# Other start addresses in SBUF for the tiles of a decoder layer: three pads of new sizes

## The chip, the cores and the metric

The kernel runs on one core of a Trainium2 chip. The metric is the time of one execution on the device, in microseconds. The core has TensorE (PE in the profile; PEld is its loading of weights), VectorE (DVE), ScalarE (ACT), GpSimd (POOL) and SyncE (SP, which here only issues DMAs). They share a memory of 128 partitions, SBUF. A tile lies at the same address in every partition, and "start" below means that address in bytes, mostly modulo 512.

## The reference

One decoder layer on 1024 tokens of width 1024, all in float32:

```python
xn = rmsnorm(x, norm_mix_w)
da_q, da_k, da_v, sw_q, sw_k, sw_v, g_da, g_sw = split_cols(xn @ w_in)
y_da = diff_attention(da_q, da_k, da_v, ...)        # 4 heads, causal, ALiBi
y_sw = sliding_window_attention(sw_q, sw_k, sw_v, sinks)   # 8 heads, window 128
merged = sigmoid(g_da) * (y_da @ w_br_da) + sigmoid(g_sw) * (y_sw @ w_br_sw)
x = x + merged @ w_mix_out
x = x + conv_ffn(rmsnorm(x, norm_ffn_w), w_up, conv_w, conv_b, w_down)   # width 2816
return rmsnorm(x, norm_final_w)
```

## The kernel before

**Products.** Every large product keeps float32's accuracy with three matmuls. Weights and activations are each cut into a high part (`wh`, `xh`) and the rest (`wl`, `xl`), and `wh` x `xh`, `wh` x `xl` and `wl` x `xh` are added in PSUM (lines 150 to 152, 276 to 278, 835 to 837, 996 and 1023). A matmul streams 512 columns of the activation, the moving operand, against 128x128 weights; the weights of the next matmul are loaded while it streams. `wh` is used by two matmuls in a row and loaded for each.

**Pairs.** Two blocks of weights are often computed together by a scheme with seven products in place of eight (P1 to P7). It needs sums of weight blocks, S1 to S4, whose two parts are the tiles `sh` and `sl`, and sums of activations, T1 to T4 (`t13h`, `t42h` and so on in the projection, `T_0h` and so on later). A11, A12 and A22 are plain weight blocks, B11, B21 and B22 plain activations (`B_0h` and so on).

**Stages**, in order: the projection (`project`), attention (`attention`, with blocks of gates between its steps, `back_half`), the merge of the two branches (in `rest`, moving operands `yh`, `yl`), the mix (`mix`, operands `mh`, `ml`), the hidden stage (`hidden`, 22 pairs of blocks) and the down projection (`down`, operands `h`).

**Where tiles lie.** Pools of tiles are stacked in SBUF from two sides. The order in which the pools are opened sets the addresses. At the very bottom of each side `run` opens a pad, a pool with one tile that nothing reads or writes (lines 180 to 182; LPAD and RPAD on line 32). From the left follow constants, `rstd`, and then the pool `wp` with the weights as they are loaded (`raw`) and their two parts (`wh`, `wl`). Behind it, also from the left, come each stage's other left-hand tiles: the sums of weights of the projection, the merge's operands, the parts of the hidden stage's activations, most parts `h` of the down projection. From the right come the activations of the projection and their sums, nearly all of attention, `mh` and `ml`, and in the hidden stage and the down projection the sums of weights and some of the activations (T42 and the pool `hpb`). Nearly all of these tiles have sizes that are multiples of 512 bytes, so the tiles of one side keep one start modulo 512.

In the program built from this kernel the tiles of `wp` and the other left-hand ones start at 192 modulo 512, those from the right at 0. Slices inside a tile keep that: weights are taken in steps of 512 bytes, activations in steps of 2048.

**Order.** Each engine works through its own list. A scheduler makes the lists when the program is built, and semaphores make an engine wait for another where one needs the other's result.

Of the kernel before, what the change touches and what calls it, by code (L numbers as in the profile page):

```python
# [10 lines left out]
F32 = mybir.dt.float32  # L11
# [6 lines left out]
P = 128  # L18
# [10 lines left out]
STORE = (1,9)  # L29
DEFER = (4,8)  # L30
N1 = 6
LPAD, RPAD = 480, 480
LAM_INIT = 0.2

HALVES = ((2,), (0, 0, 0, 0, 1, 1, 0, 0), (0, 0, 0, 0, 1, 0, 0, 1), (0, 0, 0, 0, 1, 0, 1, 0), (0, 0, 0, 1, 1, 0, 1, 0), (1, 0, 0, 1, 0, 1, 1, 0), (1, 0, 1, 1, 0, 0, 1, 0), (3,))
# [7 lines left out]
class Trunk:  # L43
# [132 lines left out]
    def run(self):  # L176
        nc, tc = self.nc, self.tc
        with ExitStack() as ctx:

            for side, n in (("left", LPAD), ("right", RPAD)):  # L180
                pad = ctx.enter_context(tc.tile_pool(name=f"pad_{side}", bufs=1, side=side))
                pad.tile([P, n // 4], F32, name=f"pad_{side}_t")
            self.cp = ctx.enter_context(tc.tile_pool(name="cp", bufs=1))
            self.st = ctx.enter_context(tc.tile_pool(name="st", bufs=4))
            self.dp = ctx.enter_context(tc.tile_pool(name="dp", bufs=1, space=DRAM))
            self.ident = self.cp.tile([P, P], F32, name="ident")
            make_identity(nc, self.ident)
            self.ones = self.cp.tile([P, 1], F32, name="ones")
            nc.gpsimd.memset(self.ones, 1.0)
            self.mhalf = self.cp.tile([P, 8], F32, name="mhalf")  # L190
            nc.gpsimd.memset(self.mhalf, -0.5)
            self.vecs = self.cp.tile([P, NVEC], F32, name="vecs")

            warm = self.cp.tile([P, 1], F32, name="warm")
            nc.scalar.activation(warm, self.ones, AF.Exp)
            nc.scalar.dma_start(self.vecs, self.vecs_d)
            self.rstd = self.cp.tile([P, T], F32, name="rstd")
            self.gd = self.dp.tile([16, P, T], F32, name="gd")
            self.x2d = self.dp.tile([8, P, T], F32, name="x2d")
            self.hd = self.dp.tile([NF, P, T], F32, name="hd")  # L200
            self.yd = self.dp.tile([8, P, T], F32, name="yd")
            self.wp = ctx.enter_context(tc.tile_pool(name="wp", bufs=2))
            self.qd = self.dp.tile([18, 2, P, T], F32, name="qd")
            self.xctx = ExitStack()
            self.xp = self.xctx.enter_context(tc.tile_pool(name="xp", bufs=1, side="right", reuse_waits="tile"))
            self.plan()
            self.project()
            self.pctx = ExitStack()
            self.psS = self.pctx.enter_context(tc.tile_pool(name="psS", bufs=2, space=PSUM, reuse_waits="tile"))
            self.psG = self.pctx.enter_context(tc.tile_pool(name="psG", bufs=2, space=PSUM, reuse_waits="tile"))  # L210
            self.psT = self.pctx.enter_context(tc.tile_pool(name="psT", bufs=2, space=PSUM, reuse_waits="tile"))
            gctx = ExitStack()
            self.gpool = gctx.enter_context(tc.tile_pool(name="gp", bufs=2, reuse_waits="tile"))
            self.attention()
            self.rest(gctx)
# [995 lines left out]
```

## Time and profile before

The median of two runs is 1365.2 us (1364.79 to 1365.61). One execution was profiled; its span, from the first to the last instruction, is 1364.3 us, and no further time of that execution is given.

| stretch of the span, us | stage | PE busy, us | PE instructions | DVE busy, us | DMA share |
|---|---|---|---|---|---|
| 0 to 252 | projection | 244.85 | 1068 | 170.09 | 0.46 |
| 252 to 509 | attention | 255.10 | 1503 | 209.25 | 0.54 |
| 509 to 598 | merge | 87.81 | 382 | 44.29 | 0.44 |
| 598 to 687 | mix | 88.83 | 387 | 52.65 | 0.42 |
| 687 to 1119 | hidden | 431.30 | 1873 | 376.18 | 0.25 |
| 1119 to 1364 | down | 237.34 | 1099 | 163.39 | 0.47 |

Matmuls overlap in the pipeline and their ends are modelled, so a busy PE isn't a PE at its peak. To see how fast matmuls follow one another, look at the starts of successive ones. In the profile's rows, a line of groups has: line, engine, operation, output <- inputs (moving operand, weights), tile, form, count, then busy us and mean ns of one, then idle time before. A line of the chain has: start, duration, engine, tile, line, count.

### The profile page before, as it was taken

To read this page: it belongs to the slowest core of one execution; us is meant where nothing else is said; L and a number is where in the kernel's file an instruction comes from. 1 tells how busy PE (TensorE), PEld (TensorE's weight loads), DVE (VectorE), ACT (ScalarE), POOL (GpSimd) and SP (SyncE) were. 2 spreads that over 40 slices of the span, in tenths; PEclk is the share of its full clock that TensorE was granted. 3 is DMA by queue.
4 is the path that set the end of the run, shared out by engine and by line. 5 is a ranking of instruction groups with operands and counts; after the bars stand their busy time and mean duration, and the time that the engine had idled before them with its cause. 6 is when DMAs were issued, how large, how long until landed. Compare 5 with 4: busy or idle time off the path is not lost.

```text
span 1364.3 us, 17160 instructions
## 1 busy us (share of the span) xinstructions
PE 1345.2 (99%) x6304; PEld 1104.3 (81%) x6304; DVE 1015.9 (74%) x1454; ACT 603.9 (44%) x942; POOL 485.5 (36%) x350
## 2 busy tenths in 40 slices
PE   8999999999999999999999999999999999999997
PEld 6888888888887778878878888888888888888887
DVE  8747775388898875455689889888988888976454
ACT  8432232276667674334444333433344335332343
POOL 0336652010102135642455565556555611131011
PEclk9999999999999999999999999999999999999999
DMA  7334343966554235334522222222222238651242
GB/s 254 139 106 173 137 147 118 271 173 178 154 132 144 82 118 220 110 124 129 165 78 93 77 78 93 67 88 78 93 77 79 85 136 316 206 179 59 93 133 84
DMA packets 62469, 179.50 MB, mean 132 GB/s; under 512 B 6832, under 2 KB 15152, under 8 KB 62384
## 3 DMA queue, kind: packets, MB, share of 16 engines
q1 hardware_dynamic: 50928, 160.98, 36.5%
q10 hardware_dynamic: 11456, 17.41, 3.5%
q8 instruction: 50, 0.82, 0.2%
q14 instruction: 35, 0.29, 0.1%
HBM read 129.61 MB, written 48.76 MB: 131 GB/s over the span
## 4 chain that ended last, share of the span: by engine, by line
PE 86%; DVE 5%; POOL 3%; DMA 3%; issue 1%; ACT 1%; POOLq 0%; SPq 0%; ACTq 0%; DVEq 0%
PE t L837 14%; PE t L836 14%; PE t L835 14%; PE d L996 3%; PE y L996 3%; PE sc L568 3%; PE g L150 3%; PE g L151 3%; PE g L152 3%; DMA gr<-gd 2%; PE sc L152 2%; PE sc L150 2%; PE sc L151 2%; PE d L1023 2%; PE y L1023 2%; POOL gr L742 2%
## 5 line engine op out<-in xcount | busy, mean ns | idle before, releaser
L970 ACT ACTIVATE c<-us,vecs 128x1024 f32<-128x1024 f32 x44 | 54.7, 1246 | 162.6 <-POOL us L965 159.1
L965 POOL TENSOR_TENSOR us<-us,rstd 128x1024 f32<-128x1024 f32 x42 | 100.9, 2420 | 54.7 <-DVE wl L131 36.4
L110 ACT CAST sh<-sf 128x1024 fp32r<-128x1024 f32 x62 | 64.7, 1047 | 108.4 <-POOL sf L97 59.7
L129 ACT CAST wh<-raw 128x1024 fp32r<-128x1024 f32 (+2 forms) x60 | 60.7, 1011 | 108.6 <-PE sc L151 33.6
L131 DVE TENSOR_TENSOR wl<-raw,wh 128x1024 fp32r<-128x1024 f32 (+2 forms) x60 | 75.8, 1263 | 41.5 <-ACT wh L129 31.6
L971 DVE SCALAR_TENSOR_TENSOR c<-us,vecs,c 128x1024 f32<-128x1024 f32 x44 | 67.2, 1530 | 52.0 <-ACT c L970 52.0
L96 POOL TENSOR_TENSOR sf<-rv 128x512 f32<-128x512 f32 x30 | 43.0, 1434 | 166.6 <-DMA rv<-in_w_up 62.6
L112 DVE TENSOR_TENSOR sl<-sf,sh 128x1024 fp32r<-128x1024 f32 x62 | 90.5, 1462 | 8.6 <-ACT sh L110 8.4
L167 POOL TENSOR_TENSOR rs<-ms,mhalf 128x8 f32<-128x8 f32 (+2 forms) x9 | 14.5, 1615 | 161.2 <-DVE ms L165 150.6
L150 PE MATMUL g<-xh,wh 128*128 128x512 f32 x176 | 70.6, 401 | 0.1
L152 PE MATMUL g<-xh,wl 128*128 128x512 f32 x176 | 70.5, 401 | 0.0
L151 PE MATMUL g<-xl,wh 128*128 128x512 f32 x176 | 70.3, 399 | 0.0
L98 POOL TENSOR_TENSOR sf<-raw,rv 128x512 f32<-128x512 f32 x30 | 41.7, 1391 | 61.1 <-DVE sl L112 61.1
L572 DVE CUSTOM_DVE_ANT_0 L<-sc,bias 128x128 f32<-128x128 f32 (+7 forms) x64 | 47.7, 751 | 17.0 <-PE sc L568 13.8
L551 POOL MEMSET aT<- 128x128 f32 x32 | 6.2, 206 | 151.8 <-PE t L597 101.3
L97 POOL TENSOR_TENSOR sf<-sf,raw 128x512 f32<-128x512 f32 x31 | 58.1, 1875 | 1.7
L573 ACT ACTIVATE L<-L,sm 128x128 f32<-128x128 f32 (+7 forms) x64 | 49.6, 778 | 20.3 <-DVE sm L572 17.7
L972 DVE SCALAR_TENSOR_TENSOR c<-us,vecs,c 128x1024 f32<-128x1024 f32 x44 | 56.1, 1278 | 0.6
L725 POOL TENSOR_TENSOR gr<-gr,rstd 128x1024 f32<-128x1024 f32 x16 | 40.4, 2528 | 41.4 <-DMA gr<-gd 41.0
L112 DVE TENSOR_TENSOR wl<-raw,wh 128x1024 fp32r<-128x1024 f32 (+1 forms) x35 | 54.8, 1565 | 0.2
L150 PE MATMUL sc<-mh,wh 128*128 128x512 f32 x128 | 50.4, 394 | 0.0
L152 PE MATMUL sc<-mh,wl 128*128 128x512 f32 x128 | 50.2, 392 | 0.0
(444 smaller groups left out, 4358.8 us busy)
## 6 DMA issues: line engine op xcount, KB each, us to landing
u<-qd SPq DMA_DIRECT2D x72, 256.0 KB, 6.4
raw<-in_w_down SPq DMA_DIRECT2D x27, 512.0 KB, 3.7
raw<-in_w_in SPq DMA_DIRECT2D x25, 512.0 KB, 3.9
hr<-hd SPq DMA_DIRECT2D x50, 256.0 KB, 5.5
raw<-in_w_up SPq DMA_DIRECT2D x23, 512.0 KB, 3.5
hd<-c SPq DMA_DIRECT2D x22, 512.0 KB, 2.8
rv<-in_w_up SPq DMA_DIRECT2D x21, 512.0 KB, 3.5
gr<-gd SPq DMA_DIRECT2D x16, 512.0 KB, 3.6
```

Source lines behind the costliest of these rows:

```text
L110: nc.scalar.copy(hi, src)
L112: nc.vector.tensor_tensor(lo, src, hi.bitcast(F32), ALU.subtract)
L131: self.lo = (eng or nc.vector).tensor_tensor(wl, raw, wh.bitcast(F32), ALU.subtract)
L150: nc.tensor.matmul(ps, wh[:, kc + o, :], ah, start=first and n == 0, stop=False)
L151: nc.tensor.matmul(ps, wh[:, kc + o, :], al, start=False, stop=False)
L152: nc.tensor.matmul(ps, wl[:, kc + o, :], ah, start=False, stop=last and n == len(kcs) - 1)
L835: nc.tensor.matmul(ps, ah[:, k, :], bh, start=first and n == 0, stop=False, skip_group_check=skip)
L836: nc.tensor.matmul(ps, ah[:, k, :], bl, start=False, stop=False, skip_group_check=skip)
L837: nc.tensor.matmul(ps, al[:, k, :], bh, start=False, stop=last and n == len(ks) - 1, skip_group_check=skip)
L965: i = (nc.vector if m % NF == 0 else nc.gpsimd).tensor_tensor(us[:, 2:], us[:, 2:], self.rstd, ALU.mult)
L971: nc.vector.scalar_tensor_tensor(c, us[:, 1:T + 1], cw[1], c, ALU.mult, ALU.add)
L996: nc.tensor.matmul(ps, v[:, n, :], x, start=n == i == 0, stop=n == len(js) - 1 and i == 2)
```

## The change

Two pads get other sizes, and a third pad is opened behind `wp`, on the left. In the program built from the changed kernel the tiles of `wp` start at 0 modulo 512, the left-hand tiles of the pools behind it at 64, those from the right at 160. Constants and `rstd` move along (`rstd` from 32 to 352). The instructions of every engine, their order and what they wait for are those of the program before; the DMAs are the same too. The pads take 1184 bytes of each partition in place of 960.

```diff
-LPAD, RPAD = 480, 480
+LPAD, MPAD, RPAD = 288, 64, 832
...
             self.wp = ctx.enter_context(tc.tile_pool(name="wp", bufs=2))
+            pad = ctx.enter_context(tc.tile_pool(name="pad_middle", bufs=1))
+            pad.tile([P, MPAD // 4], F32, name="pad_middle_t")
             self.qd = self.dp.tile([18, 2, P, T], F32, name="qd")
```

## The prediction

> **What bounds the kernel now.** First the page's busy times, its slices and its chain of work.
>
> ```profile
> span 1364.3 us, 17160 instructions
> PE 1345.2 (99%) x6304; PEld 1104.3 (81%) x6304; DVE 1015.9 (74%) x1454; ACT 603.9 (44%) x942; POOL 485.5 (36%) x350
> ...
> PE   8999999999999999999999999999999999999997
> ...
> PEclk9999999999999999999999999999999999999999
> ...
> PE 86%; DVE 5%; POOL 3%; DMA 3%; issue 1%; ACT 1%; POOLq 0%; SPq 0%; ACTq 0%; DVEq 0%
> ```
>
> TensorE is busy from the first slice to the last at a granted clock of nine tenths or more, and 86% of the chain is matmuls. So the time is the number of matmuls times the distance between the starts of two of them. That distance, which I call the cadence, is what an address could change. I read it from three stretches without a wait: two from the chain in order of time (start, us, what), one from the timeline (start, us of one).
>
> ```profile
> 1263.61 5.44 PE d L996 x24
> ```
>
> ```profile
> 1121.58 2.06 PE y L1023 x9
> ```
>
> ```profile
> 956.12 0.39 PE L835 MATMUL t<-T_1h,sh 128*128 128x512 f32 x1
> ...
> 959.62 0.39 PE L835 MATMUL t<-B_2h,sh 128*128 128x512 f32 x1
> ```
>
> All three run the same instruction, 128x512 against 128x128 weights, one weight load to each matmul. The first takes 5.44/24 = 226.7 ns, the second 2.06/9 = 228.9 ns, and in the third 15 matmuls start between the two rows: 3.50/15 = 233.3 ns. What differs is where the operands lie. While a matmul streams its moving operand, the weights of the next are loaded. I call "distance" the start of those weights minus the start of the moving operand, modulo 512 bytes; slices of a weight tile are 512 bytes apart and halves of an activation 2048, so it is the same for a whole group. In the first stretch weights and moving operand both lie at 192: distance 0. In the second the weights lie at 192 and the operand at 0: +192. In the third it is the other way round: -192. The trace thus ties the cadence to the distance; it shows only these three, and the change leaves only one of them in use.
>
> The groups by line (form, count, busy, mean ns of one) show how even this is:
>
> ```profile
> L150 PE MATMUL sc<-mh,wh 128*128 128x512 f32 x128 | 50.4, 394 | 0.0
> L152 PE MATMUL sc<-mh,wl 128*128 128x512 f32 x128 | 50.2, 392 | 0.0
> L151 PE MATMUL sc<-ml,wh 128*128 128x512 f32 x128 | 49.9, 390 | 0.2
> ...
> L837 PE MATMUL t<-t13h,sl 128*128 128x512 f32 x72 | 28.4, 394 | 0.0
> L836 PE MATMUL t<-t13l,sh 128*128 128x512 f32 x72 | 28.2, 392 | 0.0
> L835 PE MATMUL t<-t13h,sh 128*128 128x512 f32 x72 | 27.9, 388 | 0.0
> ...
> L152 PE MATMUL g<-yh,wl 128*128 128x512 f32 x64 | 24.9, 389 | 0.0
> ...
> L835 PE MATMUL t<-B_0h,wh 128*128 128x512 f32 x44 | 17.4, 395 | 0.0
> ...
> L837 PE MATMUL t<-B_0h,wl 128*128 128x512 f32 x44 | 17.2, 391 | 0.0
> L836 PE MATMUL t<-B_0l,wh 128*128 128x512 f32 x44 | 17.1, 389 | 0.0
> ```
>
> A mean here is a modelled end: rows of 389 belong to stretches of 226.7, so I take some 162 off. The mix (`mh`, +192) then runs at 230 ns, the projection's sums (`t13h`, +192) at 229, the rows at distance 0 at 227 with a run-in: the first rows of a product show 395 and 391, the later ones 389, some 228 on average. Sums against left tiles (-192) run at 233.
>
> **The change part by part.** It alters three pad sizes and adds a fourth pad that no instruction touches. The lists of the two built programs have the same instructions in the same order on every engine, the same waits and the same DMAs; only start addresses differ. So nothing is removed, queued or moved past anything. In the built programs, 5240 matmuls are 512 wide. By what streams and what is loaded beside it:
>
> - wp weights beside a right-hand operand (projection, gates, mix, A22 with T4, part of the down projection): 1818, distance +192 becomes -160.
> - wp weights beside a left-hand operand (merge, P1 and P2 of the hidden stage, most of the down projection): 1458, 0 becomes -64.
> - sums (`sh`, `sl`) on the right beside a left-hand operand: 898, -192 becomes +96.
> - sums on the left beside a right-hand operand (projection): 480, +192 becomes -96.
> - both on the right (attention, S2 with T2): 575, 0 stays 0.
>
> The other 11 are single transitions. Per nanosecond of cadence the four changed groups are worth 1.8, 1.5, 0.9 and 0.5 us. No row has any of the four new distances, so each is bounded from both sides by the stretches above: 226.7 ns below, 233.3 ns above. All four at the lower end: 1818 x 3.3 + 1458 x 1.4 + 898 x 6.3 + 480 x 2.3 ns = 6.0 + 2.0 + 5.7 + 1.1 = 14.8 us less. All four at the upper end: 6.0 + 7.6 + 0.3 + 2.1 = 16.0 us more.
>
> For the value I take, the nearest rows are those at 0 and at 192 to either side. Counted by amount alone, distance 0 has 228.1 and distance 192 has (1818 x 230 + 480 x 229 + 898 x 233)/3196 = 230.7 ns, so 0.0135 ns per byte between them. That gives 230.3 at 160, 229.4 at 96 and 229.0 at 64. The sum: 1818 x 0.3 = +0.5, 1458 x 0.9 = +1.3, 898 x -3.6 = -3.2, 480 x 0.4 = +0.2, together -1.2 us. The profiled span is 1364.3 us, 0.9 below the median of the runs, 1365.2; from the median the forecast is **1364.0 us**. I take this middle course because one group that goes nearer and one that goes farther nearly cancel; the line between two amounts is a choice, no measurement.
>
> The rest of the machine is costed at nothing. Casts, subtractions and transfers also get new starts (raw weights move from 192 to 0, attention stacks from 0 to 160), and their price is unknown in both directions. What hides it is TensorE's own 99%: of 1364.3 us it is idle for 19.1. Two casts of one size at different starts bound it:
>
> ```profile
> L110 ACT CAST sh<-sf 128x1024 fp32r<-128x1024 f32 x62 | 64.7, 1047 | 108.4 <-POOL sf L97 59.7
> L129 ACT CAST wh<-raw 128x1024 fp32r<-128x1024 f32 (+2 forms) x60 | 60.7, 1011 | 108.6 <-PE sc L151 33.6
> ```
>
> They differ by 4% (the second has smaller forms in it); 4% of 19.1 us is 0.8 us, more or less. If the cover went, 12% of the chain is DVE, POOL, DMA and ACT, 164 us, and 4% of that would be 6.5 us.
>
> **A rule against the change.** The Trainium skill, SBUF — State Buffer, section SBUF: two separate sides, has TensorE never waiting for another reader, and its bandwidth table gives weight loads a second, independent read port. By that rule addresses would be indifferent and the sum exactly zero, 1365.2 us; the stretches of 226.7 and 233.3 ns above speak against it, so I leave it 3%.
>
> **The rivals.**
>
> *Sign decides, and it gets slower.* Distances below zero cost what -192 costs now, 233.3, and those above zero what +192 costs, 229. Then the new -160 and -64 and -96 pay 1818 x 3.3 + 1458 x 5.2 + 480 x 4.3 = 6.0 + 7.6 + 2.1, and +96 gains 898 x 4 = 3.6: 12.1 us more, **1377 us**. For it: the only negative distance in the trace is the dearest, and 1458 matmuls leave the cheapest. Against it: one distance is no rule for three others. It decides as soon as the two large groups rise by 3.6/3.28 = 1.1 ns together.
>
> *All at the cheap cadence.* If 226.7 is where the reads fit best and any distance well away from 192 has it, the four groups reach it: 14.8 us less, **1350 us**. For it: the cheapest stretch is at the smallest distance, and three of the new ones are 96 or less. Against it: the run-in (395, 391, 389) shows that even distance 0 pays more until a phase is found.
>
> *The collision goes away.* Early in the kernel the same instruction pays nothing for the loads beside it:
>
> ```profile
> 11.26 0.63 PE L278 MATMUL t<-xh,wl 128*128 128x512 f32 x1
> 11.68 0.63 PE L277 MATMUL t<-xl,wh 128*128 128x512 f32 x1
> 12.11 0.63 PE L278 MATMUL t<-xh,wl 128*128 128x512 f32 x1
> ```
>
> There the starts lie 0.425 us apart, the array still at half its later rate; twice 213 ns, without the 13 to 20 ns that the later stretches have on top. So a weight load need not delay the stream. At distances where it doesn't, the four groups, 229.9 ns on average now, save 4654 x 16.6 ns = 77 us: **1288 us**, or part of it. Against it: none of the three distances seen is free at the full rate. The Trainium skill, TensorE: Matmul & The Clock Gate, section Back-to-back issue gap, gives N/2.4 + 2.5 ns, 216 ns for 512 columns; an estimate by that page would be 1300 us, and no stretch at full rate here shows it.
>
> **How the numbers follow.** Chances: the forecast, between 1356 and 1372, 0.40; slower by sign, 1372 to 1385, 0.24; all cheap, 1343 to 1356, 0.20; collision gone or partly so, below 1343, 0.12; no effect at all, 0.03, which gives the same time as the forecast; dearer than any steady stretch, 0.01. Within 2%, about what a measurement of this kernel can tell from no change, lie 1338 to 1392.5. The forecast, the sign rival, the cheap rival and no effect lie inside it; faster than that is most of the collision rival, 0.11; slower than that needs a cadence above 235 ns, 0.02. The range is 1342 to 1382: it takes in the lower end (1350) and the upper end (1381) of the unknown cadences with the 6.5 us of the other engines below and a little above, and leaves out the collision rival.
>
> **What would show it.** In the changed profile the rows of the mix (394, 392, 390), the projection's sums (394, 392, 388) and the merge (389) say the new cadence of -160, -96 and -64 at once, less 162. Right: mix near 392, merge near 391, the hidden stage's rows with `sl` or `sh` and a left operand down to some 391. The sign rival shows 394 to 396 in mix and merge; the cheap one 389 throughout; the collision rival rows below 386. TensorE's idle time should stay near 19 us, and attention's `sc<-u,u` as it is. I am wrong if idle time moves by more than 2 us, or if the cadence at an unchanged distance of 0 moves.

## The result, and the profile after

The changed kernel takes 1374.5 us, the median of two runs (1373.88 to 1375.05), against 1365.2 before: a ratio of 1.0068, with an interval of 1.0052 to 1.0084. It is slower by 9.3 us. That lies within 2% and inside my range, but I had forecast 1364.0, on the other side of the time before. The profiled execution took 1373.88 us; its span is 1372.1, 7.8 above the span before.

The page of the changed kernel: the span, the busy times, TensorE's slices and granted clock, and the shares of the chain of work by engine.

```profile
span 1372.1 us, 17160 instructions
...
PE 1355.0 (99%) x6304; PEld 1107.7 (81%) x6304; DVE 1014.1 (74%) x1454; ACT 604.1 (44%) x942; POOL 483.5 (35%) x350
...
PE   8999999999999999999999999999999999999997
...
PEclk9999999999999999999999999999999999999998
...
PE 93%; DVE 4%; issue 1%; ACT 1%; DMA 1%; POOL 0%; POOLq 0%; ACTq 0%; SPq 0%; DVEq 0%
```

The number of instructions is as before, and so is the granted clock but for the last slice. TensorE is idle for 1372.1 - 1355.0 = 17.1 us, 2.0 less than before. So it has not waited more; its matmuls follow one another more slowly. Its share of the chain is 93%, against 86% before.

The groups by line of the changed kernel (form, count, busy us and mean ns of one, idle time before):

```profile
L152 PE MATMUL sc<-mh,wl 128*128 128x512 f32 x128 | 50.8, 397 | 0.0
L151 PE MATMUL sc<-ml,wh 128*128 128x512 f32 x128 | 50.8, 397 | 0.0
L150 PE MATMUL sc<-mh,wh 128*128 128x512 f32 x128 | 50.8, 397 | 0.0
L570 PE MATMUL sc<-u,u 128*128 128x512 f32 (+2 forms) x192 | 49.6, 358 | 0.0
...
L837 PE MATMUL t<-t13h,sh 128*128 128x512 f32 x72 | 28.6, 397 | 0.0
L838 PE MATMUL t<-t13l,sh 128*128 128x512 f32 x72 | 28.5, 396 | 0.0
L839 PE MATMUL t<-t13h,sl 128*128 128x512 f32 x72 | 28.3, 393 | 0.0
```

The lines stand two further down than before, since the middle pad adds two lines. The mix showed 394, 392 and 390 before and shows 397 in all three rows now. The projection's sums showed 388, 392 and 394 and show 397, 396 and 393. Attention's `sc<-u,u`, both operands on the right at an unchanged distance, is the same 358 as before:

```profile
L568 PE MATMUL sc<-u,u 128*128 128x512 f32 (+2 forms) x192 | 49.7, 358 | 0.0
```

The cadence itself, from the chain in order of time (start, us, what) of the changed kernel, in the down projection:

```profile
1131.73 2.11 PE y L1025 x9
...
1144.38 2.10 PE y L1025 x9
...
1270.70 5.49 PE d L998 x24
```

The first is the stretch that took 2.06/9 = 228.9 ns at +192. At -160 it takes 2.11/9 = 234.4. The last took 226.7 at distance 0 and takes 5.49/24 = 228.8 at -64. The middle one is also at -64, and takes 2.10/9 = 233.3: one distance, two steady cadences. Two more stretches, from the timeline (start, us of one), are a piece of the merge (-64) and one of the hidden stage (+96):

```profile
531.01 0.39 PE L150 MATMUL g<-yh,wh 128*128 128x512 f32 x1
...
537.19 0.40 PE L150 MATMUL sc<-yh,wh 128*128 128x512 f32 x1
...
964.09 0.40 PE L837 MATMUL t<-B_0h,sh 128*128 128x512 f32 x1
...
966.20 0.40 PE L837 MATMUL t<-B_3h,sh 128*128 128x512 f32 x1
```

Between the first two rows 27 matmuls start: 6.18/27 = 228.9 ns. Between the last two, 9: 2.11/9 = 234.4.

I took the start-to-start times of all 512-column matmuls from both traces, by the distance of their operands. Times over 245 ns count as waits; those over 1 us, 5.9 us in sum in either kernel, are left out of the last row. The last column is the matmuls of the program times the change of the mean.

| group | matmuls | distance before, after | mean cadence before, after, ns | us |
|---|---|---|---|---|
| `wp` weights, right-hand operand | 1818 | +192, -160 | 229.9, 233.9 | +7.4 |
| `wp` weights, left-hand operand | 1458 | 0, -64 | 227.8, 229.5 | +2.4 |
| sums on the right, left-hand operand | 898 | -192, +96 | 233.1, 233.8 | +0.6 |
| sums on the left, right-hand operand | 480 | +192, -96 | 228.9, 233.4 | +2.1 |
| both on the right | 575 | 0, 0 | 230.7, 229.0 | -0.9 |
| what the waits have above 230 ns | | | 18.8 us, 15.4 us | -3.4 |

The sum is +8.2 us, against +7.8 in the span. The loss is in the cadence, and three fifths of the 12.5 us of the four changed groups come from the first.

### The profile page after: what moved, and what is told of

Same layout as the page of the kernel before. It is cut to its first block, busy times and chain, and to the rows that moved or that the text cites. A ratio compares the mean times of both kernels' runs of the same rounds, so it can differ in the third digit from the quotient of the medians.

```text
span 1372.1 us, 17160 instructions
## 1 busy us (share of the span) xinstructions
PE 1355.0 (99%) x6304; PEld 1107.7 (81%) x6304; DVE 1014.1 (74%) x1454; ACT 604.1 (44%) x942; POOL 483.5 (35%) x350
## 4 chain that ended last, share of the span: by engine, by line
PE 93%; DVE 4%; issue 1%; ACT 1%; DMA 1%; POOL 0%; POOLq 0%; ACTq 0%; SPq 0%; DVEq 0%
PE t L837 14%; PE t L838 14%; PE t L839 14%; PE g L150 4%; PE g L151 4%; PE g L152 4%; PE y L998 3%; PE d L998 3%; PE sc L151 3%; PE sc L152 3%; PE sc L150 3%; PE sc L570 3%; PE d L1025 2%; PE y L1025 2%; PE t L586 1%; PE sc L658 1%
## 5 line engine op out<-in xcount | busy, mean ns | idle before, releaser
L151 PE MATMUL sc<-ml,wh 128*128 128x512 f32 x128 | 50.8, 397 | 0.0
```

Of the source, the lines that this page charges most:

```text
L151: nc.tensor.matmul(ps, wh[:, kc + o, :], al, start=False, stop=False)
```

## The experiments

My theory behind the result (A) was that the cadence hangs on the relative distance alone, by a curve that I had taken for a line. The rivals were that the start itself counts, wherever the other operand lies (B), and that reads by the other engines make the difference (C). Of the two kernels without the layer, some lines are shown; the edits of the layer's variants are against the changed kernel.

**TensorE alone, in steps of 32 bytes.** One kernel with no layer in it: 48 matmuls at each of 16 distances, first in rising order (L38), then mixed (L42), then mixed with the moving operand 192 bytes further (L46), so that the label is the distance only in the first two. It was executed once.

```diff
+STEP = 32
+ORDER = (0, 5, 14, 3, 12, 7, 1, 10, 15, 6, 2, 13, 8, 11, 4, 9)
...
+        for i in range(16):
+            for k in range(N):
+                first(i % 8, i, k)
...
+            o = 48 + 256 * (k // 2 % 2)
+            nc.tensor.matmul(banks[b], wts[i][:, 0:P], mvs[k % 2][:, o:o + 512], start=k == 0, stop=k == N - 1)
```

> This kernel computes nothing of the layer: TensorE alone streams 128x512 matmuls against 16 weight tiles whose starts lie 32 bytes apart, 48 matmuls per distance, once in rising order and twice in a mixed order, the second mixed pass with the moving operand 192 bytes further on; no other engine works beside it. Theory A, the cadence depends on the distance from the moving operand to the next weights modulo 512 alone: 226.7 ns at 0, 228.9 or 233.3 at +192, 233 to 234 at -192, -160, -96 and +96, 229 to 230 at -64, and the same curve in all three passes when it is drawn over the distance. Rival B, the absolute start of a stream sets its price: flat over the weight tiles inside a pass, another level in the third pass. Rival C, the price comes from the other engines reading at the same time: flat, at 216 ns or less above it.

The chain of this kernel in order of time (start, us, what; 48 matmuls of one distance to a row). With the order above, the second pass has in these rows the distances 0, 448, 96, 384, 192, 256, 352 and 128:

```profile
198.50 10.91 PE bank L42 x48
...
220.84 10.99 PE bank L42 x48
...
231.94 11.24 PE bank L42 x48
243.30 11.16 PE bank L42 x48
...
299.84 10.98 PE bank L42 x48
...
333.58 10.89 PE bank L42 x48
344.58 11.24 PE bank L42 x48
355.94 11.16 PE bank L42 x48
```

Rows 256 bytes apart agree: 0 and 256 (10.91, 10.89), 96 and 352 (11.24 twice), 128 and 384 (11.16 twice), 192 and 448 (10.98, 10.99). The steady cadence, over the second half of each 48, for all sixteen:

| distance modulo 256 | 0 | 32 | 64 | 96 | 128 | 160 | 192 | 224 |
|---|---|---|---|---|---|---|---|---|
| ns | 226.7 | 233.3 | 233.3 | 234.4 | 232.1 to 232.8 | 233.3 | 228.9 | 233.3 |

The third pass gives the same table when 192 is taken off its labels. So the distance between the two operands counts and not where they lie; the curve repeats after 256 bytes; and no other engine works beside these matmuls, so none is needed for it. Read modulo 256, the change moved the largest group from 192, one of two dips, to 96, the dearest value; the sums on the left from 192 to 160; the sums on the right from 64 to 96; and the left-hand group from 0 to 192.

**One start for all.** All tiles at 192, every distance 0.

```diff
-LPAD, MPAD, RPAD = 288, 64, 832
+LPAD, MPAD, RPAD = 480, 0, 288
...
-            pad = ctx.enter_context(tc.tile_pool(name="pad_middle", bufs=1))
-            pad.tile([P, MPAD // 4], F32, name="pad_middle_t")
```

> All three kinds of tiles start at 192 modulo 512, so every group of matmuls has distance 0. Theory A: 228 ns for all of them, run-in counted; against before 1818 x 1.9 + 480 x 0.9 + 898 x 5.1 ns = 8.5 us less, 1357 us, with a few us open for the run-in. Rival B: the streams from the right keep a price of their own start, the ones at 192 showed 228 and 233 in before, so anything from 1360 to 1374 us. Rival C: no change from before, 1365 us.

1357.4 us, a ratio to before of 0.9937 (0.9920 to 0.9954). The mean cadence is 227.3 ns, against 229.8 before and 232.1 with the change. Rival B had at least 1360 us.

**The left part alone.** `wp` at 0 and the other left-hand tiles at 64 as in the change, the right side at 0 as before.

```diff
-LPAD, MPAD, RPAD = 288, 64, 832
+LPAD, MPAD, RPAD = 288, 64, 480
```

> One part of the change alone: the left-hand tiles as in the changed kernel (weights at 0, the others at 64), the right-hand ones at 0 as before. Distances: 0 for 1818 and 575 matmuls, -64 for 1458 and 898, +64 for 480. Theory A: 1818 x -1.9 + 1458 x +1.7 + 898 x -3.6 ns and 480 at 229 to 233: 1361 to 1364 us. Rival B, with streams at 0 cheap and at 64 dear as in the changed kernel: streams at 0 keep 229.9, streams at 64 take 231 (the mean of 229.5 and 233.8), 1458 x 3 + 898 x -2: 1368 us. Rival C: 1365 us.

1363.8 us, a ratio of 0.9986 (0.9976 to 0.9995). Two of its groups by line, the mix (now at distance 0) and the merge (-64):

```profile
L152 PE MATMUL sc<-mh,wl 128*128 128x512 f32 x128 | 49.8, 389 | 0.0
...
L152 PE MATMUL g<-yh,wl 128*128 128x512 f32 x64 | 25.2, 394 | 0.0
```

The mix gains what +192 had above 0, and the merge gives up what -64 costs. The sums on the left pay for +64 (228.9 ns in the mean before, 233.2 here), and those on the right gain from -192 to -64 (233.1 and 229.4). Nearly nothing is left.

**The right part alone.** The right side at 160, all left-hand tiles at 0.

```diff
-LPAD, MPAD, RPAD = 288, 64, 832
+LPAD, MPAD, RPAD = 288, 0, 320
...
-            pad = ctx.enter_context(tc.tile_pool(name="pad_middle", bufs=1))
-            pad.tile([P, MPAD // 4], F32, name="pad_middle_t")
```

> The other part: the right-hand tiles at 160 as in the changed kernel, the left-hand ones all at 0, weights included. Distances: -160 for 1818 and 480 matmuls, 0 for 1458 and 575, +160 for 898. Theory A: 1818 x +4.0 + 480 x +5.0 ns = 9.8 us more than before, and the 898 at +160, not seen yet, between -4 and +1 us: 1371 to 1376 us, all or more of the loss of the changed kernel. Rival B: the streams at 160 dear, those at 0 cheap, the same sign, 1370 us, so this run alone doesn't tell A from B; together with the left-only run it does, since A says that the two parts don't add up to the whole (their sum would be a distance of 0 for three groups) and B says that they do. Rival C: 1365 us.

1374.4 us, a ratio of 1.0061 (1.0046 to 1.0076). The same two groups:

```profile
L152 PE MATMUL sc<-mh,wl 128*128 128x512 f32 x128 | 50.8, 397 | 0.0
...
L152 PE MATMUL g<-yh,wl 128*128 128x512 f32 x64 | 24.9, 389 | 0.0
```

The merge is back at 389, the mix at 397 as in the change. This part alone costs as much as the whole. The times of the two parts don't show whether parts add up: 0.14% less and 0.61% more, against 0.68% more, is a gap that the intervals cover. By group they don't, since each distance has one end on either side: the sums on the right have 233.1 ns before, 229.4 with the left part, 233.8 with the right part and 233.8 with both.

**TensorE alone, in steps of 4 bytes.** Again without the layer: steady groups at 17 distances in rising and in falling order (L49), weights in turn at 0 and 96 (L52), and 384 or 256 columns at 0 and at 96 (L55).

```diff
+FINE = (0, 4, 8, 12, 16, 20, 24, 28, 176, 184, 188, 196, 200, 208, 240, 248, 252)
...
+        def turns(b, k):
+            nc.tensor.matmul(banks[b], pair[k % 2], mv(k), start=k == 0, stop=k == N - 1)
+        def short(b, i, k, n):
+            nc.tensor.matmul(banks[b][:, 0:n], i, mv(k, n), start=k == 0, stop=k == N - 1)
```

> Again nothing of the layer: TensorE alone, 48 matmuls at each of 17 distances that are no multiples of 32 bytes (steps of 4 near 0, some near 192 and near 256), in two orders; then weights at distance 0 and 96 in turns; then 384 and 256 columns. The first bench showed a curve that repeats after 256 bytes. Theory A: only the weights loaded next count, so in the part with turns the matmuls that use the tile at distance 0 (the next load is at 96) are the long ones. Rival: the weights in use count, then it is the other way round. If each load costs a fixed time on top of the stream, 13.3 ns at distance 0 and 21.1 at 96 as at 512 columns, then 384 columns take 173.3 and 181.1 ns, 256 columns 120.0 and 127.8; if it is a share of the stream, 170.0 and 175.8, 113.3 and 117.2. On distances below 32 bytes: if the price is set by 16-byte lines, 4 to 12 stay at 226.7 and 16 to 28 form a second level; if by the exact byte, each has its own value. No distance below 226.7 is expected.

The chain of this kernel in order of time: the distances 0, 12, 16 and 28 in rising order, then 28, 16 and 12 in falling order, then one of the two groups with weights in turn, and the four shorter groups (384 columns at 0 and 96, 256 columns at 0 and 96).

```profile
24.35 10.90 PE bank L49 x48
...
57.83 11.20 PE bank L49 x48
69.15 11.20 PE bank L49 x48
...
102.98 10.88 PE bank L49 x48
...
316.72 10.88 PE bank L49 x48
...
350.42 10.89 PE bank L49 x48
361.48 11.21 PE bank L49 x48
...
406.44 11.04 PE bank L52 x48
...
428.88 8.34 PE bank L55 x48
...
437.40 8.33 PE bank L55 x48
...
445.85 5.76 PE bank L55 x48
451.73 5.65 PE bank L55 x48
```

28 bytes are as cheap as 0 in both orders, 12 are dear in both, and 16 are dear in one order and cheap in the other: 233.3 and 226.7 ns steady. The same holds for 252. Between neighbouring multiples of 4 the cadence jumps; there is no slope to draw a line through, and no level that holds for 16 bytes, as I had thought possible.

Two more expectations missed. With 384 columns, 0 and 96 are alike (8.34 and 8.33, 173.3 ns steady), and with 256 columns 96 is even the cheaper one (117.3 against 120.0). The table above therefore holds for 512 columns only. And weights in turn were to tell whether the load of the next weights or the weights in use make the distance:

```profile
L52 PE MATMUL bank<-xl,aUB 128*128 128x512 f32 x48 | 18.9, 393 | 0.0
...
L52 PE MATMUL bank<-xh,aOB 128*128 128x512 f32 x48 | 18.8, 392 | 0.0
```

By these groups of the same kernel, `aOB` at 0 and `aUB` at 96 differ by 1 ns, where their steady groups differ by 7.7; both run at some 230 ns, about the mean of the two. That question stays open. Within one product of the layer all weights have one distance, so it moves none of the sums here.

**The right side at 256.** All left-hand tiles at 0, those from the right at 256: the distances are 0 modulo 256 and far from 0 modulo 512.

```diff
-LPAD, MPAD, RPAD = 288, 64, 832
+LPAD, MPAD, RPAD = 288, 0, 224
...
-            pad = ctx.enter_context(tc.tile_pool(name="pad_middle", bufs=1))
-            pad.tile([P, MPAD // 4], F32, name="pad_middle_t")
```

> Left-hand tiles and weights at 0, right-hand ones at 256: distances 256 for 2298 and 898 matmuls, 0 for the others. Theory A with a curve that repeats after 256 bytes: as with one start for all, 227.3 ns, 1357 us. If the curve repeated after 512 only, 256 would be one more distance away from 0, at some 233 ns: 1818 x 3.4 + 480 x 4.4 us/1000 more than before, 1371 us or so.

1356.7 us, a ratio of 0.9939 (0.9924 to 0.9954). The mix, from its groups by line:

```profile
L152 PE MATMUL sc<-mh,wl 128*128 128x512 f32 x128 | 49.8, 389 | 0.0
```

256 bytes apart costs as little as 0 in the layer too. By a line in the amount modulo 512 it would have been the dearest.

**The change with the right side at 320.** One number differs from the changed kernel. Modulo 256 the large group is back at 192 and both groups of sums are at 0, while the left-hand group keeps -64.

```diff
-LPAD, MPAD, RPAD = 288, 64, 832
+LPAD, MPAD, RPAD = 288, 64, 160
```

> The changed kernel with one number undone: weights at 0, other left-hand tiles at 64, right-hand ones at 320 in place of 160. Distances modulo 256: 192 for 1818 and 1458 matmuls, 0 for 898, 480 and 575. Theory A with the bench's steady cadences (228.9 at 192, 226.7 at 0) and the run-in seen in the kernels (229.4 and 227.3): 1818 x -0.5 + 1458 x 1.6 + 898 x -5.8 + 480 x -1.6 ns = 4.6 us less than before, 1361 us, 13 us less than the changed kernel. If it is 64 or the fourth pad that costs, it stays near 1370.

1360.7 us, a ratio of 0.9966 (0.9954 to 0.9977). Its groups:

```profile
L150 PE MATMUL sc<-mh,wh 128*128 128x512 f32 x128 | 50.2, 392 | 0.0
L152 PE MATMUL sc<-mh,wl 128*128 128x512 f32 x128 | 49.7, 388 | 0.0
...
L837 PE MATMUL t<-t13h,sh 128*128 128x512 f32 x72 | 28.0, 389 | 0.0
```

The mix is down from 397 to 392 and 388, the projection's sums to 389. One step of the right side, from 160 to 320, takes back all the loss of the change and some 4 us more.

**Everything at 0.** The control for one start at another place.

```diff
-LPAD, MPAD, RPAD = 288, 64, 832
+LPAD, MPAD, RPAD = 288, 0, 480
...
-            pad = ctx.enter_context(tc.tile_pool(name="pad_middle", bufs=1))
-            pad.tile([P, MPAD // 4], F32, name="pad_middle_t")
```

> All three kinds of tiles at 0 modulo 512. Theory A: distance 0 as with all at 192, so 1357 us within 1.5. If the absolute start counts too, through the transfers or the other engines, another time: a gain of some us would point to transfers that start on a multiple of 256 bytes.

1356.6 us, a ratio of 0.9938 (0.9923 to 0.9953), the same as with everything at 192. It is faster than both kernels: by 0.6% than the one before, by 1.3% than the changed one (1.0068/0.9938). Groups by line of this kernel:

```profile
L152 PE MATMUL sc<-mh,wl 128*128 128x512 f32 x128 | 49.8, 389 | 0.0
...
L837 PE MATMUL t<-B_0h,wl 128*128 128x512 f32 x44 | 18.6, 422 | 0.6 <-DVE wl L112 0.3
```

The mix is at 389. The second row, 391 without any idle time before the change, now shows waits for DVE and a mean of 422: the faster matmuls run into the next limit. What the long start-to-start times have above 230 ns rises from 18.8 us to 22.9. The mean cadence fell by 2.6 ns, 13.5 us over 5240 matmuls; 4.1 of them went into such waits, and the span is 8.8 us shorter.

## Why the prediction was wrong

**What bounds the kernel: right.** The time is the number of matmuls times the cadence, and the cadence goes with the distance between the two operands. The six variants of the layer follow it, and the first bench shows it with TensorE alone. The four groups, their counts and their old and new distances were right too. (Of the pads, two change their size and a third is added, not three and a fourth.)

**The step that failed: the line between two amounts.** I gave 192 a mean of 230.7 for both signs and drew a line from 0 to it. It gave 230.3 at 160, 229.4 at 96 and 229.0 at 64. Measured were 233.9 at -160, 233.4 at -96, 233.8 at +96 and 229.5 at -64: only the last fits, and that by luck. The merge's stretch at 228.9 is about what the line said, because -64 happens to be the same place as +192 modulo 256. The three stretches I had (226.7, 228.9, 233.3) were two dips and one ordinary value. Averaging +192 with -192 hid that: taken modulo 256 they are 192 and 64, two different places. By the terms of the sum: +0.5 forecast for the large group, measured +7.4; +1.3 for the left-hand one, +2.4; -3.2 for the sums on the right, +0.6; +0.2 for those on the left, +2.1. The first bench's steady cadences in place of the line would have given 16.3 us more for the four groups, against 12.5 measured: the right direction, and too much, above all since the large group had 229.9 before in place of the steady 228.9.

**The bounds held nearly.** 226.7 is the lowest steady value in any run. 233.3 is exceeded, by 234.4 at distances 96 and 352. The upper end, 16.0 us more, was never reached, since the left-hand group rose by 1.7 ns and not by the 5.2 of the sum. The range, 1342 to 1382, took the result in.

**The rival "sign decides"** gave 1377 us and the right direction. Its mechanism is not what happens. It priced +96 at 229, and that is as dear as -96 (233.8 and 233.4); it priced -64 at 233.3, and that has 229.5 in the mean. Its two errors nearly cancelled.

**"All at the cheap cadence"** failed for the new distances. "Any distance well away from 192" is refuted: 226.7 was found only at 0 and 256, at 28 in both orders, and at 16 and 252 in one. The gain itself exists: with all distances at 0 modulo 256 the kernel takes 1357 us, not 1350, since the lower end left out run-ins and the waits that then appear.

**"The collision goes away"** is not seen: of the 32 different distances tried with 512 columns at full rate, none was below 226.7 ns, some 13 above the 213 ns that this rival took for the columns alone. By the Trainium skill, TensorE: Matmul & The Clock Gate, section Back-to-back issue gap, an estimate for 512 columns is 216 ns, for a matmul by itself and not for a stream of weight loads and matmuls; no run here shows it for these matmuls with a weight load each.

**"No effect"** is refuted by the first bench: with TensorE alone the same 48 matmuls take 10.89 to 11.24 us by distance. The Trainium skill, SBUF — State Buffer, section SBUF: two separate sides, has TensorE never waiting on another reader and weight loads with a read port of their own. Addresses are not indifferent all the same: here up to 7.7 ns of a matmul follow from where weights and operand lie to each other.

**The rest of the machine at nothing: nearly right.** TensorE's idle time went from 19.1 to 17.1 us, just at the 2 us that I had named as the limit, and towards less. By the table, the waits gave back 3.4 of the 12.5 us. That slower matmuls cover more of the other engines' work would explain it, but it is not shown: with the right part alone the matmuls were nearly as slow, and these waits still had 18.1 us, against 18.8 before.

**The cadence at an unchanged distance of 0: it moved**, which I had named as a sign of being wrong. Attention's row stayed at 358, but the 575 matmuls with both operands on the right moved by -1.6 ns in the mean. With the right part alone they had 231.0, at the same addresses modulo 512 as in the change (229.0), so their addresses don't explain it. The trace puts the move in one product of the hidden stage, S2 with T2, 12 matmuls for each of the 22 pairs. Here is one of them, from its first start to the first start of the next product (start, us of one), before and with the change:

```profile
894.34 0.39 PE L835 MATMUL t<-T_0h,sh 128*128 128x512 f32 x1
...
897.11 0.39 PE L835 MATMUL t<-T_0h,sh 128*128 128x512 f32 x1
```

```profile
900.22 0.39 PE L837 MATMUL t<-T_0h,sh 128*128 128x512 f32 x1
...
902.94 0.40 PE L837 MATMUL t<-T_0h,sh 128*128 128x512 f32 x1
```

The 12 take 2.77 us before and 2.72 with the change. Leaving out the first two pairs, they have some 230.5 ns from start to start before and 226.6 with the change, and in each kernel it goes with the distance of the 12 matmuls just ahead of them: 230.4 to 231.2 behind -192, -64 and +160, 226.6 behind +96, 0 and 256. In the 12 shown for before, only the last two take 227 ns each. So a short product at distance 0 can be dear for nearly its whole length, and the distance of a group alone doesn't give its cadence. That makes 1 us here, all of this group's share.

## What to carry to other kernels

Where TensorE is busy all the time and loads weights for every matmul, the start addresses of weights and moving operand relative to each other are worth measuring, and for 512-column float32 matmuls here the same start modulo 256 bytes was best of those tried in the layer. Don't draw a line through two or three addresses: measure the curve with the engine alone, a matter of one short kernel, before pricing a move. When two values carry opposite signs and different costs, treat them as different places instead of averaging them.

## What was not expected of the hardware

The cadence of 512-column matmuls repeats after 256 bytes of distance, from 226.7 ns at 0 over 233.3 to 234.4 at 96, with a second dip of 228.9 at 192. It is not smooth: 12 bytes cost 233.3 and 28 bytes 226.7.

One distance can have two steady cadences. At -64 the changed kernel keeps 228.8 in one stretch and 233.3 in another; at 16 and 252 bytes the order of the groups decided between 226.7 and 233.3. What sets which of the two is found was not tried. The distance just ahead is not all of it: of two stretches of the changed kernel at -64 that both follow one at -160, the first keeps 233.3 over 72 matmuls, and the second goes over to 226, 229 and 232 in turn within a few.

The dearness of 96 is gone with 384 and 256 columns. At distance 0 the three lengths, 120.0, 173.3 and 226.7 ns, lie on one line of 53.3 ns per 128 columns. By that line, an estimate from these three values, 512 columns alone take 213.3 ns, about half the 0.425 us of the early stretch, and some 13 ns remain for each matmul whatever its length. Why the distance acts as it does, and why with this period, stays open.
